# A hybrid decoder step: the reciprocal of lambda's squared modulus made early and kept

## The chip, the cores and the metric

One core of one Trainium2 chip runs the kernel, which is written by hand for its five engines (TensorE, VectorE, ScalarE, GpSimd, and SyncE, which issues loads). The metric is the device time of one execution in microseconds, as the median of three runs. Nothing is computed on the host.

## The reference, cut to what matters

The program is one inference step of a two-layer decoder for 256 prompt tokens and 8 x 4 sample tokens, together 288 columns. Layer 0 has forgetting attention and an S5 state-space layer side by side behind one input projection, then an output projection and a SwiGLU feed-forward part. Layer 1 has a pooling mixer and a feed-forward part. The change concerns the constants of S5:

```python
def s5_mixer(u, h0_re, h0_im, lam_re, lam_im, log_dt, b_re, b_im, c_re, c_im, d, w_glu, b_glu):
    dt = jnp.exp(log_dt.astype(F32))[:, None]
    lr, li = lam_re.astype(F32), lam_im.astype(F32)
    mag = jnp.exp(lr * dt)
    ar, ai = mag * jnp.cos(li * dt), mag * jnp.sin(li * dt)
    den = lr * lr + li * li
    zr = ((ar - 1.0) * lr + ai * li) / den
    zi = (ai * lr - (ar - 1.0) * li) / den
    ...
    # bb = z * b; a scan x <- a x + bb u over the tokens; y = Re(c x) + d u
    z = jax.nn.gelu(y)
    out = z * jax.nn.sigmoid(z @ w_glu.astype(F32) + b_glu.astype(F32))
```

There are 64 groups of 64 states, so den, zr and zi are arrays of 128 partitions x 32 on the chip.

## The kernel before, in words

**The weight stream.** All large products take their weights from a ring. SyncE loads a unit of 256 KB into one of four raw buffers; ScalarE casts it to float32r (wh, line 124), VectorE makes the rest (wl = raw - wh, line 125), and TensorE makes three products for each tile (lines 162 to 164: wh with xh, wh with xl, wl with xh). A unit of layer 0's projections has 12 such matmuls over 288 columns. There are four buffers of wh and wl, and the split of a unit is put into the queues three units ahead of its products.

**Ticks.** After the products of each unit the program, as it is written out, calls tick(): each generator in the list side goes one step further and puts its instructions into the engines' queues there. So the order of each engine's queue is fixed by hand: a table W says how many ticks ("units of products") pass between two steps that wait for one another, and ticks(n) lets n of them pass. Engines work through their queues in order; an instruction whose operands are late holds up all behind it on that engine. Where a part needs a flag that is not set yet, until(...) calls ticks with no products between (forced ticks).

The order of the stream in layer 0 is: u (4 groups of 8 units, ticks 1 to 32), f (33), q and k (8 groups of 8, ticks 34 to 97), v (4 groups of 8, to 129), GLU (16 units), w_out's S5 half of two groups (8 units), until the prompt's and the samples' attention is done, then the rest of w_out.

**S5.** gen_s5_prep makes the constants, nearly all on GpSimd, in small steps of 128 x 32: exp32 of log_dt and of lambda times dt, sine and cosine by polynomials, powers of a, then den, am = ar - 1, zr, zi. Then VectorE makes z times b (the tile tab at line 194), and the powers of a times b and c (powers). TensorE makes the lag matrix (L585), which goes through eight small DMAs (L607) into mt. gen_s5_main brings u into place, makes the states (L726, then GpSimd steps and fill), and the outputs (L784), writes y to zscr and loads it again as zs (L805), from which the GLU takes its input zt. gen_s5_direct makes the part of y within a chunk from mt.

Counted in the code, the steps of before fall on these ticks:

| step | tick |
|---|---|
| first S5 step (exp32 of log_dt) | 1 |
| den and am put into GpSimd's queue | 6 |
| reciprocal of den put into VectorE's queue | 15 |
| zr, zi and the step factors put into GpSimd's queue | 16 |
| first products with b (tab) in VectorE's queue | 19 |
| states begin (flag g), end of them (flag gdone) | 48, 68 |
| fill begins | 83 |
| mt there (flag m), direct part done (flag direct) | 88, 93 |
| prompt heads begin, two chains of four heads, 14 ticks a head | 103, 105 |
| load of zs issued (flag z) | 125 |
| GLU asks for z | 129 |
| transposes of heads 6 and 7; their products with v | 152, 154; 157, 159 |
| w_out asks for the attention: six forced ticks | 155 to 161 |

The flag direct also starts the prompt's attention (through gen_cb and its ticks). The samples' attention follows q and k: its first three tiles of key pages (two loads of 256 KB each) are asked for at gdone, one more each second tick from 77 on; pages of v in the same way from 125 on.

small(...) and t2(...) hand out tiles; t2 is a ring of five buffers of one tag. In exp32 the tile named den is scratch, too.

Of the kernel before, what the change touches and what calls it, by code (L numbers as in the profile page):

```python
# [15 lines left out]
# units of products that pass between steps that wait for one another  # L16
W = dict(n0a=3, n0b=0, n0c=0, n0d=2, rec=9, s5a=3, gq=0, xw=0, qk0=2, qk1=2, qk2=0, qk3=1, qk4=0, f=2, m=4, lag=2,
# [44 lines left out]
def hybrid_step(ctx, tc, I, O):  # L62
# [9 lines left out]
    # ---------------------------------------------------------------- helpers  # L72
# [24 lines left out]
    class Ring:  # L97
        """weights: loaded, split into two float32r parts that add up to them, handed out in order"""
# [45 lines left out]
    def group(ring, ks, kpu, rhs, nb=2, m=128, evac=None, ps=None, first=True, last=True, pre=None, n=NT):  # L144
        """nb blocks of m output features: sum over the tiles of ks of weights times rhs"""
        if ps is None:
            ps = psum.tile([128, 2, 512], F32, name="m", tag="m", bufs=2)
        pb = ps if isinstance(ps, list) else [ps[:, b] for b in range(2)]
        c = nb * m
        ks = list(ks)  # L150
        for u in range(0, len(ks), kpu):
            if pre is not None:
                pre(u // kpu)
            h, l = ring.take()
            for j, k in enumerate(ks[u:u + kpu]):
                xh, xl = rhs(k)
                for b in range(nb):
                    o = pb[b][:m, :n]
                    w0 = j * c + b * m
                    st = first and u + j == 0  # L160
                    sp = last and u + j == len(ks) - 1
                    T.matmul(o, h[:, w0:w0 + m], xh, start=st, stop=False)  # L162
                    T.matmul(o, h[:, w0:w0 + m], xl, start=False, stop=False)  # L163
                    T.matmul(o, l[:, w0:w0 + m], xh, start=False, stop=sp)  # L164
            ring.ahead(ring.look)
            tick()
            if u + kpu >= len(ks) and evac is not None:
                pending.append(lambda: evac(ps))
        return ps
# [10 lines left out]
    def use_table(func):  # L180
        """Ln and Exp from the set that has both"""
        if func in (AF.Ln, AF.Exp):
            if table[0] != "ln_exp":
                S.preload_act_table_set("natural_log_exp_and_others")
            table[0] = "ln_exp"
        else:
            table[0] = func
# [14 lines left out]
    # ------------------------------------------------------ constants, inputs  # L202
# [13 lines left out]
    # ------------------------------------------------------------- rms norms  # L216
    class Norm:
        """xh + xl = x * w in two parts, and rstd, which products are scaled by"""
# [62 lines left out]
    def rsqrt_steps(srcs, n, out):  # L281
        """out[:, i] = (srcs[i] / n + eps) ** -0.5"""
        c = len(srcs)
        v = t2("v", shape=(128, c, NT))
        y = t2("y", shape=(128, c, NT))
        q = t2("q", shape=(128, c, NT))
        for i, s in enumerate(srcs):
            V.tensor_scalar(v[:, i, :], s, 1.0 / n, EPS, op0=OP.mult, op1=OP.add)
        yield
        act(y, v, AF.Ln)  # L290
        act(y, y, AF.Exp, scale=-0.5)
        S.activation(q, y, AF.Square)
        yield
        V.scalar_tensor_tensor(q, q, -0.5, v, op0=OP.mult, op1=OP.mult)
        if isinstance(out, list):
            out.append(q)
            out = q
        V.scalar_tensor_tensor(out, q, 1.5, y, op0=OP.add, op1=OP.mult)

    # ======================================================= layer 0: mixers  # L300
# [5 lines left out]
    def w_units(ap, kpu):  # L306
        """ap: [groups, 128, k tiles, c]"""
        out = []
        for g in range(ap.shape[0]):
            for k in range(0, ap.shape[2], kpu):  # L310
                a = ap[g, :, k:min(k + kpu, ap.shape[2])]
                out.append(a.rearrange("p k c -> p (k c)"))
        return out

    def first_two(units, order=(0, 1, 2, 4, 5, 6, 3, 7)):
        """the units of two groups of 16 k tiles, interleaved, 4 tiles each time"""
        n = len(units) // 8
        u = [units[i * n:i * n + n] for i in range(8)]
        return sum([u[i] for i in order], [])
# [28 lines left out]
    def gen_n0():  # L348
        """squares, their sums, and the first outputs, which wait for them"""
        yield from ticks(W["n0a"])  # L350
        sq = None
        for j in range(8):
            if sq is not None:
                add(n0.acc, n0.acc, sq)
            sq = n0.square(j, False)
            yield
        G.dma_start(bcd[:, 0], I["s5b"])
        G.dma_start(bcd[:, 1], I["s5c"])
        add(n0.acc, n0.acc, sq)
        n0.combine(V)  # L360
        yield from ticks(W["n0b"])
        n0.finish_pe(psum)
        yield from ticks(W["n0c"])
        for _ in n0.finish_steps():
            yield from ticks(W["n0d"])
        yield
        flags.add("rstd")
        for f, ps in early:
            f(ps)
            yield  # L370
        flags.add("early")
# [7 lines left out]
    # ------------------------------------------------ S5: constants of layer  # L379
# [6 lines left out]
    def gstt(out, a, c, b, op0, op1):  # L386
        """out = (a op0 c) op1 b"""
# [5 lines left out]
    def exp32(out, x):  # L393
        """exp on [128, 32]: 2**n times a polynomial, to the last bits"""
# [13 lines left out]
    def gen_s5_prep():  # L408
        lre, lim, ldt = (par[:, o:o + 32] for o in (P_LRE, P_LIM, P_LDT))
        dt, th, mag = small("dt"), small("th"), small("mag")  # L410
        exp32(dt, ldt)
        yield
        mul(mag, lre, dt, G)
# [3 lines left out]
        # sin and cos of th: the angle brought into [-pi, pi], then a polynomial  # L417
# [43 lines left out]
        am, den, t, u = small("am"), small("den"), small("zt"), small("zu")  # L461
        zr, zi = small("zr"), small("zi")
        mul(den, lre, lre, G)
        mul(t, lim, lim, G)
        add(den, den, t, G)
        G.tensor_scalar(am, ar, -1.0, None, op0=OP.add)
        yield from ticks(W["rec"])
        V.reciprocal(den, den)
        yield
# [3 lines left out]
        mul(zr, t, den, G)  # L473
# [3 lines left out]
        mul(zi, t, den, G)  # L477

        def steps(name, a):
            """the factors of a step, laid out as the states are: quarters, parts, pairs"""  # L480
# [44 lines left out]
        def powers(dst, src, j0, pr, neg):  # L525
            """dst[:, part, pair, j] = src * a**(j0 + j); the imaginary part negated if neg"""
# [47 lines left out]
        # lags: kall[64 h2 + c', quad, g2, (j, c)]  # L574
# [58 lines left out]
    # ------------------------------------------------------------- u, and f  # L633
# [49 lines left out]
    def gen_s5_main():  # L683
# [10 lines left out]
        # states: initial ones of the samples, zeros, ends of the chunks of the prompt  # L694
# [8 lines left out]
        def step(eng, dst, src, a, sh):  # L703
            """dst += a * src; sh: how many of them, of how many pairs"""
# [13 lines left out]
        for q in range(4):  # L718
# [14 lines left out]
            # within blocks of 4 chunks  # L733
# [6 lines left out]
        # the ends of the blocks, one after the other  # L740
# [8 lines left out]
        def fill(eng, q):  # L749
            """what the blocks start from, carried through their chunks"""  # L750
# [57 lines left out]
    def gen_s5_direct():  # L808
        """the part of y within a chunk"""
# [28 lines left out]
    # ------------------------------------------------ f: the logs of forgetting  # L838
# [41 lines left out]
    # ---------------------------------------------------------------- q and k  # L880
# [40 lines left out]
    # ----------------------------------------------------- attention: samples  # L921
# [99 lines left out]
    def gen_prep(hg):  # L1021
        """probabilities of the samples, keys first, on the columns of their products"""
# [76 lines left out]
    # ----------------------------------------------------- attention: prompt  # L1099
    def gen_prompt(e):  # L1100
        yield from need("cb")
        yield from ticks(W["ps0"] * e)
        for h in range(e, NH, 2):
# [28 lines left out]
            # keys 0: queries 0, queries 1; keys 1: queries 1  # L1132
# [31 lines left out]
    # -------------------------------------------------------------------- v  # L1164
# [46 lines left out]
    # ------------------------------------------------------------------- glu  # L1211
# [34 lines left out]
    # ----------------------------------------------------------------- w_out  # L1246
# [31 lines left out]
    # =================================================================== ffn  # L1278
# [69 lines left out]
    # ============================================================== pooling  # L1348
    # the windows are sums over tokens: they are taken after the products, of
    # columns 0 .. 287 and, of what the state brings to a window, 288 .. 319  # L1350
# [57 lines left out]
    def before_last():  # L1408
        """before the last products of the ffn of layer 0"""
# [76 lines left out]
    def gen_pool_out():  # L1486
        """the last inputs of the pooling, which are outputs too"""
# [13 lines left out]
    def pool_and_first(h_evac):  # L1501
        """the products of the pooling, among them the first two groups of the ffn"""
# [53 lines left out]
def layouts(inp):  # L1556
# [21 lines left out]
    def gp(v):  # L1578
        """[64 groups, 64 states, ...] -> [128, 32, ...]"""
# [26 lines left out]
    def blocks(w, c):  # L1606
        """[K, M] -> [M / c, 128, K / 128, c]"""
# [59 lines left out]
```

## Time and profile before

| | |
|---|---|
| median of 3 runs | 2233.71 us (2233.02 to 2234.71) |
| span of the profiled execution | 2232.2 us |
| TensorE matmuls busy | 2176.1 us, 97% |
| VectorE busy | 1251.3 us, 56% |
| ScalarE busy | 911.6 us, 41% |
| GpSimd busy | 244.7 us, 11% |
| DMA | 375.50 MB, mean 168 GB/s |

The profile is of one execution. A busy share is an average over the whole span; what one place costs is read from the timelines of that place. A row of a timeline gives the start in us from the start of the span, the duration in us, the engine, the line of the code, the operation with the tiles that it writes and reads, and in brackets how long its engine stood idle before it and what ended that. In rows PE is TensorE, DVE is VectorE, ACT is ScalarE, POOL is GpSimd, SP is SyncE; a q behind the name is the engine's queue of DMA issues. PEclk is the granted clock as a share of 2.4 GHz. Ends of matmuls are modelled.

### The profile page before, as it was taken

To read this page: it belongs to the slowest core of one execution; us is meant where nothing else is said; L and a number is where in the kernel's file an instruction comes from. 1 tells how busy PE (TensorE), PEld (TensorE's weight loads), DVE (VectorE), ACT (ScalarE), POOL (GpSimd) and SP (SyncE) were. 2 spreads that over 40 slices of the span, in tenths; PEclk is the share of its full clock that TensorE was granted. 3 is DMA by queue.
4 is the path that set the end of the run, shared out by engine and by line. 5 is a ranking of instruction groups with operands and counts; after the bars stand their busy time and mean duration, and the time that the engine had idled before them with its cause. 6 is when DMAs were issued, how large, how long until landed. Compare 5 with 4: busy or idle time off the path is not lost.

```text
span 2232.2 us, 40924 instructions
## 1 busy us (share of the span) xinstructions
PE 2176.1 (97%) x16936; PEld 2138.3 (96%) x16936; DVE 1251.3 (56%) x1616; ACT 911.6 (41%) x1302; POOL 244.7 (11%) x321
## 2 busy tenths in 40 slices
PE   8998999999999999999999996899999999999999
PEld 7987988999999999999999996899999999999999
DVE  6987656655554544554554569655554455445443
ACT  5454545444333333333333353433333333333332
POOL 8365200100000000000000046200000000000000
PEclk9999999999999999999999999999999999999999
DMA  6638487555555555555555642455556555555554
GB/s 201 170 106 198 133 250 253 186 189 170 168 163 167 161 171 164 168 161 171 163 167 159 202 150 86 158 169 162 168 158 169 168 168 162 169 164 168 159 170 140
DMA packets 136571, 375.50 MB, mean 168 GB/s; under 512 B 22337, under 2 KB 26129, under 8 KB 136097
## 3 DMA queue, kind: packets, MB, share of 16 engines
q1 hardware_dynamic: 122864, 357.15, 53.1%
q10 hardware_dynamic: 11728, 11.27, 1.6%
q0 software_dynamic: 1792, 4.47, 0.7%
q8 instruction: 132, 2.16, 0.4%
q14 instruction: 55, 0.44, 0.1%
HBM read 363.42 MB, written 8.76 MB: 167 GB/s over the span
## 4 chain that ended last, share of the span: by engine, by line
PE 88%; DVE 5%; DMA 3%; POOL 2%; ACT 1%; issue 1%; ACTq 0%; SPq 0%; DVEq 0%
PE m L164 28%; PE m L162 28%; PE m L163 28%; DVE wb L197 1%; DVE wl L125 1%; PE s L784 1%; POOL stt L390 1%; DMA raw<-in_wqk_dram 1%; DMA zs<-zscr 0%; ACT wh L124 0%; DVE wb L194 0%; PE s L726 0%; PE a L585 0%; DMA raw<-in_wv_dram 0%; DMA raw<-in_w_dram 0%
## 5 line engine op out<-in xcount | busy, mean ns | idle before, releaser
L125 DVE TENSOR_TENSOR wl<-raw,wh 128x1024 fp32r<-128x1024 f32 (+2 forms) x758 | 808.1, 1071 | 793.3 <-ACT wh L124 790.2
L124 ACT CAST wh<-raw 128x1024 fp32r<-128x1024 f32 (+2 forms) x769 | 691.2, 903 | 940.0 <-PE m L163 751.7
L162 PE MATMUL m<-xh,wh 128*128 128x288 f32 (+1 forms) x3312 | 985.2, 297 | 19.0 <-ACT xh L234 12.6
L164 PE MATMUL m<-xh,wl 128*128 128x288 f32 (+1 forms) x3312 | 982.9, 297 | 16.3 <-DVE wl L125 10.4
L163 PE MATMUL m<-xl,wh 128*128 128x288 f32 (+1 forms) x3312 | 982.2, 297 | 0.0
L162 PEld LDWEIGHTS m<-xh,wh 128*128 128x128 f32 (+1 forms) x3312 | 623.9, 188 | 28.0 <-ACT xh L234 13.1
L164 PEld LDWEIGHTS m<-xh,wl 128*128 128x128 f32 (+1 forms) x3312 | 624.2, 188 | 20.4 <-DVE wl L125 13.0
L163 PEld LDWEIGHTS m<-xl,wh 128*128 128x128 f32 (+1 forms) x3312 | 624.5, 189 | 1.5 <-DVE xl L235 0.5
L164 PE MATMUL m<-gh,wl 128*128 128x288 f32 x1408 | 415.8, 295 | 0.0
L163 PE MATMUL m<-gl,wh 128*128 128x288 f32 x1408 | 415.5, 295 | 0.0
L162 PE MATMUL m<-gh,wh 128*128 128x288 f32 x1408 | 414.1, 294 | 0.0
L164 PEld LDWEIGHTS m<-gh,wl 128*128 128x128 f32 x1408 | 264.4, 188 | 0.0
L162 PEld LDWEIGHTS m<-gh,wh 128*128 128x128 f32 x1408 | 264.4, 188 | 0.0
L163 PEld LDWEIGHTS m<-gl,wh 128*128 128x128 f32 x1408 | 264.4, 188 | 0.0
L191 ACT ACTIVATE s<-t 128x288 f32<-128x288 f32 x88 | 39.1, 445 | 169.2 <-DVE t L194 169.2
L1359 POOL DMA_DIRECT2D out_plo_dram<-es x1 | 0.6, 577 | 779.8 <-DMA es<-in_spool_dram 779.8
L194 DVE TENSOR_TENSOR t<-s,t 128x288 f32<-128x288 f32 x88 | 40.3, 457 | 46.4 <-ACT s L191 46.4
L194 DVE TENSOR_TENSOR t<-m,rstd 128x576 f32<-128x576 f32 x88 | 65.9, 749 | 0.0
L1313 DVE TENSOR_TENSOR gl<-t,gh 128x288 fp32r<-128x288 f32 x88 | 40.3, 458 | 44.0 <-ACT gh L1312 44.0
L197 DVE TENSOR_TENSOR x<-m,x 128x576 f32<-128x576 f32 x72 | 54.0, 750 | 8.6 <-PE m L164 8.6
L1312 ACT CAST gh<-t 128x288 fp32r<-128x288 f32 x88 | 38.2, 434 | 46.1 <-DVE t L194 46.1
L197 POOL TENSOR_TENSOR acc<-acc,sq 128x576 f32<-128x576 f32 x20 | 31.7, 1583 | 196.9 <-ACT sq L244 186.6
(338 smaller groups left out, 1490.8 us busy)
## 6 DMA issues: line engine op xcount, KB each, us to landing
raw<-in_w_dram SPq DMA_DIRECT2D x472, 512.0 KB, 4.0
raw<-in_w_dram SPq DMA_DIRECT2D x64, 384.0 KB, 3.2
raw<-in_wqk_dram SPq DMA_DIRECT2D x64, 256.0 KB, 3.2
raw<-in_wout_dram SPq DMA_DIRECT2D x64, 256.0 KB, 3.2
raw<-in_wu_dram SPq DMA_DIRECT2D x32, 256.0 KB, 3.8
pg<-in_kc_dram SPq DMA_DIRECT2D x32, 256.0 KB, 3.7
raw<-in_wv_dram SPq DMA_DIRECT2D x32, 256.0 KB, 3.4
pg<-in_vc_dram SPq DMA_DIRECT2D x28, 256.0 KB, 3.9
```

Source lines behind the costliest of these rows:

```text
L124: S.copy(h[:, :n], t[:, :n])
L125: self.share().tensor_tensor(l[:, :n], t[:, :n], h[:, :n], OP.subtract)
L162: T.matmul(o, h[:, w0:w0 + m], xh, start=st, stop=False)
L163: T.matmul(o, h[:, w0:w0 + m], xl, start=False, stop=False)
L164: T.matmul(o, l[:, w0:w0 + m], xh, start=False, stop=sp)
L191: S.activation(out, x, func, **kw)
L194: eng.tensor_tensor(out, a, b, OP.mult)
L197: eng.tensor_tensor(out, a, b, OP.add)
L390: G.tensor_scalar(t, a, c, None, op0=op0)
L784: T.matmul(ps[64 * h2:64 * h2 + 64, 72 * d:72 * d + 72], p0[k, pair, r, 16:80], xt[k, 0:72, q, r, pair - 8 * q], start=r == 0, stop=r == 1)
L1312: S.copy(gs[c][0][:, i, :], t[:, 1, :])
L1313: V.tensor_sub(gs[c][1][:, i, :], t[:, 1, :], gs[c][0][:, i, :])
```

## The change

The squares and the sum that make lambda's squared modulus move from the end of GpSimd's chain to its head, ahead of the first exp32, into a tile of their own (rden) with a scratch tile from t2 (sqi). The reciprocal moves with them: VectorE's instruction is put in its queue in the second step of gen_s5_prep, and its result is kept until zr and zi need it. The step between the reciprocal and zr goes (one tick less), and W["rec"], the ticks that pass ahead of zr, becomes 13 in place of 9. Comments and docstrings are dropped as well, which changes no instruction.

```diff
-W = dict(n0a=3, n0b=0, n0c=0, n0d=2, rec=9, s5a=3, gq=0, xw=0, qk0=2, qk1=2, qk2=0, qk3=1, qk4=0, f=2, m=4, lag=2,
+W = dict(n0a=3, n0b=0, n0c=0, n0d=2, rec=13, s5a=3, gq=0, xw=0, qk0=2, qk1=2, qk2=0, qk3=1, qk4=0, f=2, m=4, lag=2,
...
     def gen_s5_prep():
         lre, lim, ldt = (par[:, o:o + 32] for o in (P_LRE, P_LIM, P_LDT))
+        rden, sqi = small("rden"), t2("sqi", shape=(128, 32))
+        mul(rden, lre, lre, G)
+        mul(sqi, lim, lim, G)
+        add(rden, rden, sqi, G)
         dt, th, mag = small("dt"), small("th"), small("mag")
         exp32(dt, ldt)
         yield
+        V.reciprocal(rden, rden)
         mul(mag, lre, dt, G)
         exp32(mag, mag)
...
         ar, ai = ap[:, 1, 0, :], ap[:, 1, 1, :]
-        am, den, t, u = small("am"), small("den"), small("zt"), small("zu")
+        am, t, u = small("am"), small("zt"), small("zu")
         zr, zi = small("zr"), small("zi")
-        mul(den, lre, lre, G)
-        mul(t, lim, lim, G)
-        add(den, den, t, G)
         G.tensor_scalar(am, ar, -1.0, None, op0=OP.add)
         yield from ticks(W["rec"])
-        V.reciprocal(den, den)
-        yield
         mul(t, am, lre, G)
         mul(u, ai, lim, G)
         add(t, t, u, G)
-        mul(zr, t, den, G)
+        mul(zr, t, rden, G)
         mul(t, ai, lre, G)
         mul(u, am, lim, G)
         G.tensor_tensor(t, t, u, OP.subtract)
-        mul(zi, t, den, G)
+        mul(zi, t, rden, G)
```

## Rows read from the trace of the kernel before

**Rows 1.** The page of the profiled execution, its head.

```profile
span 2232.2 us, 40924 instructions
```

**Rows 2.** Windows around the reciprocal: busy us (instructions), clock, DMA share, GB/s.

```profile
37.15:42.05 4.90, 4.89 (x38) 4.66 (x36) 0.00 (x0) 1.64 (x3) 4.13 (x16) 1.00 0.22 68
42.05:46.98 4.93, 0.00 (x0) 0.00 (x0) 0.95 (x3) 0.00 (x0) 4.36 (x15) 0.97 0.00 0
46.98:50.00 3.02, 3.02 (x12) 3.02 (x13) 2.99 (x8) 0.00 (x0) 2.69 (x8) 0.50 0.75 221
```

**Rows 3.** VectorE's timeline: start, us, line, operation, idle before and releaser.

```profile
46.03 0.35 DVE L468 RECIPROCAL den<-den 128x32 f32<-128x32 f32 x1 [8.89 <-POOL den L197]
46.30 0.63 DVE L125 TENSOR_TENSOR wl<-raw,wh 128x512 fp32r<-128x512 f32 x1
...
52.20 0.69 DVE L194 TENSOR_TENSOR tab<-bcd,zr 128x512 f32<-128x512 f32 x1
```

**Rows 4.** Timelines of ScalarE and TensorE, 312 to 327 us.

```profile
312.95 0.38 ACTq L805 DMA_DIRECT2D zs<-zscr  x1
...
323.91 3.25 ACT L1219 CAST zt<-zs 128x512 fp32r<-128x512 f32 x5 [1.74 <-PE a L1059]
...
319.21 0.65 PE L1059 MATMUL a<-pg,vtp 128*32 128x128 f32 x16
...
325.24 0.40 PE L162 MATMUL m<-zt,wh 128*128 128x288 f32 x1 [0.58 <-ACT zt L1219]
```

**Rows 5.** DMA from 309 to 326 us: whole mean, then issues (us to landing).

```profile
DMA packets 2719, 4.26 MB, mean 251 GB/s; under 512 B 197, under 2 KB 1221, under 8 KB 2718
...
raw<-in_wglu_dram SPq DMA_DIRECT2D x5, 256.0 KB, 5.8
pg<-in_vc_dram SPq DMA_DIRECT2D x5, 256.0 KB, 4.5
zs<-zscr ACTq DMA_DIRECT2D x1, 1152.0 KB, 10.9
```

**Rows 6.** DMA from 165 to 210 us, the same view.

```profile
DMA packets 7833, 9.04 MB, mean 201 GB/s; under 512 B 3728, under 2 KB 3728, under 8 KB 7797
...
mt<-kall ACTq DMA_DIRECT2D x2, 128.0 KB, 6.9
```

**Rows 7.** Waits from 171 to 208 us: total us, times, longest.

```profile
ACT wh L124 <- DMA raw<-in_wqk_dram: 15.3, 6, 5.0
...
PE s L899 <- DVE sl L893: 3.9, 1, 3.9
...
DVE tms L755 <- POOL car L759: 2.6, 1, 2.6
```

**Rows 8.** Timelines of TensorE and ScalarE, 380 to 390 us.

```profile
383.60 0.27 PE L1134 MATMUL s<-cst,sm 128*128 128x128 f32 x1
...
385.52 0.59 PE L1142 MATMUL s<-sm,vtp 128*128 128x256 f32 x2
...
384.19 0.47 ACT L1138 COPY sm<-s 128x384 f32<-128x384 f32 x1
```

**Rows 9.** GpSimd's timeline, 2 to 51 us.

```profile
2.88 0.22 POOL L397 TENSOR_SCALAR am<-par 128x32 f32<-128x32 f32 x1 [2.41 <-DMA par<-in_par_dram]
...
11.68 0.50 POOL L391 TENSOR_TENSOR dt<-stt,ei 128x32 f32<-128x32 f32 x1
...
12.68 0.32 POOL L397 TENSOR_SCALAR am<-mag 128x32 f32<-128x32 f32 x1
...
24.10 0.50 POOL L391 TENSOR_TENSOR mag<-stt,ei 128x32 f32<-128x32 f32 x1
...
46.20 0.77 POOL L357 DMA_DIRECT2D bcd<-in_s5b_dram  x1
...
50.57 0.25 POOL L194 TENSOR_TENSOR zi<-zt,den 128x32 f32<-128x32 f32 x1
```

**Rows 10.** DMA from 40 to 70 us, issues (us to landing).

```profile
bcd<-in_s5b_dram POOLq DMA_DIRECT2D x1, 512.0 KB, 4.0
```

## Prediction

> **What bounds the kernel now.** The profiled execution spans 2232.2 us [rows 1], 1.5 us under the median of the timed runs (2233.71). I make the sum against the span and add 1.5 at the end. A difference of 0.2%, 4.5 us, is about what a measurement of this kernel can tell from no change.
>
> I read the page first: TensorE is the bound nearly everywhere, so only the few places where it stands still can give or take time. Then I went through TensorE's gaps with the chain of waits beside them, up to the feed-forward part that begins near 400 us (behind it no gap is long and the S5 work is over). Four places matter.
>
> First, the reciprocal. In the windows [rows 2] the reader sees three stretches: TensorE full, then 4.93 us with no matmul at all, then 12 matmuls in 3.02 us at granted clock 0.50, the lower of its two levels (1.2 GHz). At full clock 38 matmuls fill 4.90 us, so 12 take 1.55 us. The VectorE line shows why [rows 3]: the reciprocal stood 8.89 us at the head of VectorE's queue, for GpSimd's sum of squares, which comes last in GpSimd's chain. Behind it stood the split of unit 19, which TensorE needed. The place costs 4.93 + (3.02 - 1.55) = 6.4 us.
>
> Second, the end of the S5 path [rows 4]. The load of zs is issued at 312.95, lands 10.9 us later [rows 5], the casts start at 323.91 and the first GLU product at 325.24 after a gap of only 0.58. So the S5 path is just in time: zs lands as TensorE runs out of v products.
>
> Third, 171 to 208 us: the DMA engines are saturated (201 GB/s over 165 to 210 us [rows 6]), ScalarE waits 15.3 us for raw weights, and TensorE waits 3.9 us for one split of a q/k square [rows 7]. Fourth, the start of w_out's attention half, behind the products with v at 385.52 [rows 8].
>
> **The change, part by part.** The sum of squares moves to the head of GpSimd's chain. A step of this size takes 0.22 to 0.50 us there [rows 9]; three go in at the head and three go out at the tail, so the chain's end stays. The reciprocal itself (0.35 us [rows 3]) now stands in tick 2, behind work that needs far more time than GpSimd's three steps; even if nothing hid it, 0.35 us is its price. I take 0. The scratch tile sqi takes one place in a ring of five whose tile of five places earlier is long read: 0. So the 8.89 us wait goes, and with it up to 6.4 us at this place.
>
> The second edit is the one to weigh. Formerly 9 ticks, then the reciprocal, then one more step: GpSimd's zr/zi chain stood in tick 16 and VectorE's first product with it (tab) in tick 19. Now 13 ticks pass and no step of its own for the reciprocal: tick 19 and tick 22. Everything behind in S5 moves by three ticks: m from 88 to 91, direct 93 to 96, z 125 to 128; the prompt heads, which start on direct, move with it. The weight stream does not move, and GLU still asks for z in tick 129. So the load of zs, which had four more units of v products as its cover, has one left.
>
> I therefore follow the S5 path, not TensorE, from tab to the GLU.
>
> (a) When tab starts. Without the stall TensorE ends unit 18 at 42.05 and runs on at 1.6 us a unit (12 matmuls); unit 25, the last split ahead of tab, ends at 42.05 + 7 x 1.6 = 53.2, and VectorE reaches tab near 48 (unit 25 takes the buffer of unit 21, which TensorE ends at 42.05 + 4.8 = 46.9; a cast and a split of 0.63 us [rows 3] follow). But tab needs zr and bcd. GpSimd issues the first bcd load at 46.20 and it lands 4.0 us later, 50.2; zi is there at 50.57 + 0.25 = 50.8 [rows 9, 10]. These do not come earlier through the change, since they stand behind the whole chain. They may come later: the chain's stretch from 37.15 to 46.20 now runs beside a busy VectorE, where before VectorE stood still (0.00 busy from 37.15 to 42.05 [rows 2]). The two passes of the same exponential give the price: from the am row at 2.88 to the end of dt, 9.3 us, from the am row at 12.68 to the end of mag, 11.9 us [rows 9], 28% more, with VectorE much busier in the second. On 9.05 us that is up to 2.5; I take 2.0. Then tab starts at 52.2, where it started before (52.20). Shift 0, bounds -2.0 (no slowing) and +0.5. So of the 8.89 us VectorE keeps a new wait of some 4 us for GpSimd and bcd. Unit 26's split follows the two products, near 54.3, 1.1 us after TensorE ended unit 25: a small gap returns, already inside this term.
>
> The Trainium skill speaks against the change here (SBUF — State Buffer, section Who interferes with whom): a VectorE instruction with two SBUF inputs and a GpSimd instruction that reads SBUF exclude one another for a whole instruction. The two passes above agree in direction. If each of some six splits in the stretch held GpSimd up for its full 0.63 us, the chain would end 3.8 us later in place of 2.0, an estimate from that page, and the time would be 2236.7 in place of 2234.9.
>
> (b) From tab to the issue of zs there are 106 ticks before and after, with as many products, the same S5 and prompt work. What stands in ticks 126 to 128 in place of 19 to 21 is denser: sample products with v pages, 0.65 us each [rows 4], one every second tick: 1.5 x 0.65 = +1.0. Bounds 0 and +2.
>
> (c) In the saturated stretch the mt writes, 6.9 us for 128 KB [rows 6], and the first burst of key pages move by three ticks, but the later page loads do not (they follow q and k). About 1.5 tiles of two 256 KB loads more fall into it: 0.77 MB at 201 GB/s, 3.8 us if all of it shows, nothing if the ticks ahead of it absorb them. It is nearer to nothing, since only part of the stretch stops TensorE: +0.8.
>
> (d) zs now lands beside fewer weight and page loads. Before, some 7 of the 11 loads of 256 KB in that window ran beside its 1152 KB at 251 GB/s [rows 5]. Each load less saves 0.26 MB / 251 GB/s = 1.0 us. Those already in flight stay, the ring fills its four raw buffers all the same; I take one, -1.0, bounds -4 and 0.
>
> (e) The w_out wait. Heads 6 and 7 have their transposes in ticks 152 and 154, ahead of the last product unit's tick 155, and their products with v in forced ticks behind it. Three ticks later all of the transposes, copies and products stand behind the last unit. After the last product the row at 385.52 has to wait for a transpose and its copy: 384.19 - 383.60 = 0.59 from one to the other, and 0.47 for the copy [rows 8], with a tenth of handing on 1.2 us. Bounds 0 and +2.6 (with twelve matmuls at the lower clock behind it, another 1.4).
>
> (f) The q/k square that waited 3.9 us stood behind the first carries of fill, which waited for GpSimd [rows 7]. Heads of q/k do not move, fill moves three ticks, so they part. But ScalarE was short of weights in the same stretch (15.3 us), so little of it is free: -0.8; bounds 0 and -5.4 (the 3.9 and 1.5 for twelve matmuls at the lower clock behind it, as at 47 us).
>
> Sum: 0 + 1.0 + 0.8 - 1.0 + 1.2 - 0.8 = +1.2. The 6.4 us at the reciprocal are won, and paid back by TensorE in front of the GLU: it comes there some 5 us earlier and waits for zs, 5 to 7 us in place of the 0.58 of [rows 4]. Span 2232.2 + 1.2 = 2233.4, median 2233.4 + 1.5 = **2234.9**.
>
> **Rivals.** One, faster: the gain is kept. Either zs comes much sooner, or TensorE's lead lets the collision of (f) vanish. For it: zs alone would need 1.18 MB / 251 GB/s = 4.7 us, and the wait of (f) is real. Against it: the weights in flight, and the starved ScalarE. At the full bound of (f), 4.6 us less than my value, and (d) at -3, 2 us less, the median is 2234.9 - 6.6 = 2228.3. It decides from the point where GLU's first product starts before 319.5.
>
> Two, slower: the page loads meet the mt writes. Place: VectorE's and ScalarE's wait for raw weights between 171 and 208 us. Price: (c) at its bound, 3.0 over my value, and (f) gone, 0.8, and zs as slow as before, 1.0, since the late pages then run into it: 2234.9 + 4.8 = 2239.7. It decides once ScalarE's waits for raw weights in this stretch grow from 15.3 to about 19 us.
>
> Three: the reciprocal waits as before, in tick 2, and nothing is removed. It would need GpSimd's first three steps to be late; they need only the load that the row at 2.88 waited for. Then the stall at 42 us stays, and the shift costs three ticks at the GLU; from 312.95 to 325.24 there are five units [rows 4], 2.5 us each, so 7.4 us, and with (e) 2242. I give it under 1 in 50.
>
> **How the numbers follow.** Forecast (paid back, within 0.2%) 0.62; rival one 0.16; rivals two and three together 0.22. So faster 0.16, same 0.62, slower 0.22. The range leaves out about a tenth on each side and reaches to the first two rivals: 2228.3 to 2239.7.
>
> **What will show it.** Step one is right if no reciprocal waits on GpSimd near 46 us and TensorE runs through 42 to 47 at full clock. (a) is right if tab starts between 50.2 and 52.7 and waits for zr or bcd. The payback is right if the first GLU product starts within 3 us of 325.24 with a gap of 5 us or more ahead of it. (e) shows as a gap between the last ssmh product and the first att product. I am wrong if the GLU starts near 319 (gain kept), or near 330 (S5's stretch became longer); the places to look are then [rows 4] and [rows 7].

## The result, and the profile after

The changed kernel takes 2246.47 us in the median of 4 runs (2243.78 to 2249.63), against 2233.36 us before: ratio 1.006, 95% interval 1.0049 to 1.0072. It is slower by some 13 us, and outside the range that was forecast. The profiled execution took 2247.39 us, 13.4 us of span more than [rows 1]:

```profile
span 2245.6 us, 40926 instructions
PE 2183.6 (97%) x16936; PEld 2143.6 (95%) x16936; DVE 1250.4 (56%) x1616; ACT 913.8 (41%) x1302; POOL 245.8 (11%) x321
```

The wait that was to go is gone. VectorE's timeline after, beside [rows 3]:

```profile
11.60 0.35 DVE L417 RECIPROCAL rden<-rden 128x32 f32<-128x32 f32 x1
46.80 0.69 DVE L125 TENSOR_TENSOR wl<-raw,wh 128x512 fp32r<-128x512 f32 x1 [0.89 <-ACT wh L124]
55.24 0.69 DVE L194 TENSOR_TENSOR tab<-bcd,zr 128x512 f32<-128x512 f32 x1 [7.74 <-DMA bcd<-in_s5b_dram]
55.86 0.69 DVE L194 TENSOR_TENSOR tab<-bcd,zi 128x512 f32<-128x512 f32 x1
56.47 0.69 DVE L125 TENSOR_TENSOR wl<-raw,wh 128x512 fp32r<-128x512 f32 x1
```

The reciprocal no longer waits, but VectorE stands 7.74 us before tab in place of 8.89 before the reciprocal, and the next split is again what TensorE needs. Windows of the profile after, beside [rows 2] (busy us and instructions by engine, then clock, DMA share, GB/s):

```profile
core 0: us, PE busy (x) PEld busy (x) DVE busy (x) ACT busy (x) POOL busy (x), PEclk, DMA share, GB/s
42.00:46.00 4.00, 4.00 (x32) 4.00 (x32) 2.82 (x7) 1.35 (x3) 3.49 (x7) 1.00 0.83 268
57.22:60.30 3.08, 3.08 (x13) 3.08 (x14) 3.08 (x5) 0.00 (x0) 2.92 (x6) 0.50 0.44 126
```

TensorE runs through the place of the old stall at full clock, stands still ten microseconds later, and comes back at the lower clock (1.2 GHz), 13 matmuls in 3.08 us. GpSimd's timeline after says why, beside [rows 9]:

```profile
3.37 0.25 POOL L197 TENSOR_TENSOR rden<-rden,sqi 128x32 f32<-128x32 f32 x1
3.71 0.22 POOL L397 TENSOR_SCALAR am<-par 128x32 f32<-128x32 f32 x1
13.99 0.31 POOL L391 TENSOR_TENSOR dt<-stt,ei 128x32 f32<-128x32 f32 x1
28.00 0.67 POOL L391 TENSOR_TENSOR mag<-stt,ei 128x32 f32<-128x32 f32 x1
51.38 0.77 POOL L357 DMA_DIRECT2D bcd<-in_s5b_dram  x1
54.80 0.25 POOL L194 TENSOR_TENSOR zi<-zt,rden 128x32 f32<-128x32 f32 x1
```

The chain begins 0.8 us later, is 4 us late at mag, and issues bcd at 51.38 where it was 46.20. TensorE's timeline after, its three long waits:

```profile
57.22 0.61 PE L164 MATMUL m<-xh,wl 128*128 128x288 f32 x1 [4.40 <-DVE wl L125]
188.13 0.73 PE L998 MATMUL a<-pg,qm 128*32 128x256 f32 x8 [4.53 <-POOL xt L711]
334.96 0.61 PE L162 MATMUL m<-zt,wh 128*128 128x288 f32 x1 [5.65 <-ACT zt L1219]
```

The second is the first product with a key page; the third is the GLU waiting for zs, 9.7 us later than in [rows 4]. ScalarE's timeline after, the way of z:

```profile
324.38 0.38 ACTq L805 DMA_DIRECT2D zs<-zscr  x1
333.71 4.38 ACT L1219 CAST zt<-zs 128x512 fp32r<-128x512 f32 x8 [6.50 <-DMA zs<-zscr]
```

The load of zs goes out 11.4 us later than in [rows 4], and takes 9.3 us to the first cast in place of 11.0. From the first product with att, that is, with the attention's output in w_out, the two kernels run alike again: 1846.2 us to the end after, 1845.5 before.

### The profile page after: what moved, and what is told of

The parts are those of the page before. It is cut to its first block, busy times and chain, and to the rows that moved or that the text cites. A ratio compares the mean times of both kernels' runs of the same rounds, so it can differ in the third digit from the quotient of the medians.

```text
span 2245.6 us, 40926 instructions
## 1 busy us (share of the span) xinstructions
PE 2183.6 (97%) x16936; PEld 2143.6 (95%) x16936; DVE 1250.4 (56%) x1616; ACT 913.8 (41%) x1302; POOL 245.8 (11%) x321
## 4 chain that ended last, share of the span: by engine, by line
PE 86%; DVE 5%; POOL 3%; DMA 2%; ACT 1%; issue 1%; SPq 0%; ACTq 0%; DVEq 0%; POOLq 0%
PE m L162 28%; PE m L164 28%; PE m L163 28%; DVE wl L125 1%; DVE wb L197 1%; PE s L784 1%; POOL xt L711 1%; POOL stt L390 1%; DMA raw<-in_w_dram 1%; ACT wh L124 1%; DMA pg<-in_vc_dram 0%; DVE wb L194 0%; POOL tms L707 0%; DMA zs<-zscr 0%; DMA raw<-in_wqk_dram 0%
## 5 line engine op out<-in xcount | busy, mean ns | idle before, releaser
L164 PE MATMUL m<-xh,wl 128*128 128x288 f32 (+1 forms) x3312 | 984.8, 297 | 13.4 <-DVE wl L125 9.5
L164 PEld LDWEIGHTS m<-xh,wl 128*128 128x128 f32 (+1 forms) x3312 | 626.3, 189 | 17.4 <-DVE wl L125 11.9
```

## The experiments

The table gives, for each profiled execution, the starts of three rows of the timelines (tab, issue of zs, first GLU product with the wait ahead of it, first product with att) and the median of its timed runs; the ratio to before, with its interval, stands at each run below.

| kernel | tab | zs issued | GLU (wait) | att | median us |
|---|---|---|---|---|---|
| before | 52.20 | 312.95 | 325.24 (0.58) | 386.74 | 2233.36 |
| changed | 55.24 | 324.38 | 334.96 (5.65) | 399.39 | 2246.47 |
| early_rec10 | 53.65 | 314.90 | 327.11 (0.50) | 388.57 | 2233.98 |
| shift_alone | 56.24 | 325.67 | 336.76 (6.17) | 401.35 | 2249.38 |
| late_back3 | 52.65 | 316.56 | 328.67 (0.36) | 389.86 | 2236.51 |
| cb5 | 53.18 | 323.64 | 334.77 (6.57) | 397.89 | 2245.56 |
| no_acc_adds | 52.15 | 322.37 | 333.83 (6.53) | 397.32 | 2248.42 |
| rec16 | 54.02 | 316.47 | 328.11 (7.19) | 394.94 | 2244.32 |
| rec16_back6 | 54.28 | 309.48 | 323.19 (2.00) | 384.93 | 2232.24 |
| best13 | 50.37 | 316.63 | 329.20 (0.86) | 390.36 | 2235.76 |
| best_rec10 | 49.43 | 311.33 | 323.87 (0.82) | 385.05 | 2231.20 |
| best10_pg | 49.61 | 313.56 | 326.28 (1.01) | 387.86 | 2232.59 |

### Each edit alone

**early_rec10**: the early reciprocal without the shift (S5 in the ticks of before).

```diff
-rec=13
+rec=10
```

> The early reciprocal alone: 10 ticks in place of 13, so that zr stands in tick 16 and tab in tick 19, as in the kernel before. Theory A (the loss is S5 standing three ticks later in a weight stream that has no lead over it by the time it counts): z is back in tick 125, the first GLU product starts within 4 us of 325, and the time is 2231 to 2238; VectorE waits at tab for zr and bcd from about 44 us on. Theory B (the loss is GpSimd's chain, which now ends 5 us later and sets S5's start in data; ticks do not matter): tab at 55, GLU near 335, 2243 to 2247. On the chain itself: if it is VectorE's work beside it that makes it late, it ends at 47 to 49 us here, since VectorE stands from 44 on; if it is the three steps at the head alone, it ends at 51 as in the changed kernel.

Measured: 2233.98 us (11 runs), ratio 0.9999 (0.999 to 1.0008), as theory A has it. VectorE's timeline of early_rec10:

```profile
53.65 0.69 DVE L194 TENSOR_TENSOR tab<-bcd,zr 128x512 f32<-128x512 f32 x1 [10.35 <-POOL zi L194]
```

The early reciprocal alone is worth nothing that can be measured: VectorE waits at tab in place of the reciprocal, and TensorE then waits 7.66 us for the next split. From the changed kernel this one differs in three ticks alone, and the 13 us of loss are gone. On the chain neither reading came true: it ends at 50.0, between the two.

**shift_alone**: the kernel before, its late reciprocal kept, with three ticks more ahead of tab.

```diff
-s5a=3
+s5a=6
```

> The kernel before with its late reciprocal, and three more ticks between zr and tab, so that tab stands in tick 22 and all of S5 behind it three ticks later. The stall of 8.9 us at the reciprocal stays, GpSimd's chain ends at 46 as before. Theory A: 2242 to 2248, the first GLU product at 332 to 337. Theory B: chain and zr as before, so 2232 to 2236.

Measured: 2249.38 us (4 runs), 1.0076 (1.0061 to 1.0091). TensorE's and VectorE's timelines of shift_alone:

```profile
46.83 0.61 PE L164 MATMUL m<-xh,wl 128*128 128x288 f32 x1 [6.02 <-DVE wl L125]
45.88 0.35 DVE L468 RECIPROCAL den<-den 128x32 f32<-128x32 f32 x1 [10.15 <-POOL den L197]
336.76 0.61 PE L162 MATMUL m<-zt,wh 128*128 128x288 f32 x1 [6.17 <-ACT zt L1219]
```

The old stall is there, and the GLU's new wait too. The shift alone costs at least as much as the whole change (the two intervals overlap): with early_rec10 this shows that the shift is the loss.

**late_back3**: the changed kernel, three ticks given back ahead of S5's outputs and ahead of the prompt heads.

```diff
-p=9, cb=8
+p=6, cb=5
```

> The changed kernel, with three ticks taken out of S5's later waits (6 in place of 9 between the direct part and the outputs; 5 in place of 8 in front of the prompt's heads), so that z is in tick 125 and the prompt heads are in ticks 103 and 105 again, while tab stays in tick 22. Theory A: the GLU's wait of 5.7 us goes, first GLU product at 324 to 329, 2232 to 2238. Theory B: the outputs wait for their data instead, GLU near 333 to 335, 2242 to 2247.

Measured: 2236.51 us (12 runs), 1.0018 (1.0009 to 1.0027). 10 of the 13 us come back with the program at the head left as it was: the loss is where z and the heads stand in the order. **cb5** gives back the heads' ticks alone (cb=5):

> The changed kernel with the prompt heads' start three ticks earlier (5 in place of 8 ticks behind the direct part), so that they stand in ticks 103 and 105 again; z stays in tick 128. Theory A: the part between the first GLU product and the first product of w_out with att, 61.5 us before and 64.4 with the change, is 61 to 62 again, and the time is 2 to 4 us below the change: 2242 to 2245. If the part stays at 64 the heads are not what w_out waits for, and the time stays at 2246.

Measured: 2245.56 us (4 runs), 1.0058 (1.0043 to 1.0074). From the first GLU product to the first with att it takes 63.1 us, before 61.5, changed 64.4, so theory A's 61 to 62 is missed and little of the loss is the heads'. cb5 and late_back3 differ in p alone, and have tab at 53.18 and 52.65: with z three ticks earlier its load goes out 7.1 us sooner and the time is 9 us shorter. So late_back3's gain is nearly all that of p, thus of z.

### The head: does the late chain decide?

**den_vector**: the two squares and the sum on VectorE.

```diff
-        mul(rden, lre, lre, G)
-        mul(sqi, lim, lim, G)
-        add(rden, rden, sqi, G)
+        mul(rden, lre, lre)
+        mul(sqi, lim, lim)
+        add(rden, rden, sqi)
```

> The changed kernel, with the two squares and their sum on VectorE in place of GpSimd (VectorE stands idle at that time), so that GpSimd's chain has neither the three steps at its head nor at its tail. Theory A1 (the head steps make the chain late: they push the exponentials by 0.85 us into a stretch in which VectorE is busy, and more grows out of it): the first exponential starts at 2.9 in place of 3.7, the chain ends at 46 to 48.5 in place of 48.9 to 51.4, tab starts at 50 to 52.5, TensorE's stall near 57 shrinks from 4.4 to under 2, and the time is 2238 to 2244, since S5 still stands three ticks late. Theory A2 (the lateness comes only from VectorE no longer standing still after 37): the chain ends only about 0.8 earlier, 48.1 to 50.6, and the time is as with the change.

Measured: 2245.88 us (4 runs), 1.006 (1.0045 to 1.0076). The chain starts at 2.81 again and is 1.0 us late at mag, not 4, but am stands at 49.72, still 3.8 us late: what is lost behind mag is lost without the three steps too. The time is as theory A2 has it, and TensorE still waits 3.32 us near 57.

**no_acc_adds**: the changed kernel without six of the seven additions n0.acc += sq on VectorE; so part of the norm's sum is left out. It ran once.

```diff
-            if sq is not None:
-                add(n0.acc, n0.acc, sq)
```

> The changed kernel without six of the seven sums of squares of the first norm on VectorE (sums of two tiles in SBUF, 0.8 us each, 18 to 31 us), so the norm's sum lacks them. If VectorE's two-input work slows GpSimd's steps beside it, the second exponential (dt to mag), 13.9 to 14.4 us with the steps at the head, takes 11 to 12.5, and the chain ends 1.5 to 3.5 us earlier, at 46 to 49. If GpSimd's pace is its own, both stay: 13.9 to 14.4, chain end 48.9 to 51.4. The time is not the point: 2238 to 2246.

Measured: 2248.42 us. The second exponential takes 11.9 us (dt's end to mag's; changed 14.4, before 12.4), am is at 47.83, the earliest of ten executions in which GpSimd does the squares, and tab starts at 52.15, as before. TensorE waits only 2.33 us there. Yet the GLU comes at 333.83 after 6.53 us, and the time of this one run is no better. cb5 against early_rec10 says the same with more runs: tab at 53.18 and 53.65, and 2245.56 against 2233.98 us. So tab's lateness is not what costs.

**rec16**: three ticks more still, so that VectorE comes to tab when bcd is there.

```diff
-rec=13
+rec=16
```

> The changed kernel with 16 ticks in place of 13: tab in tick 25, z in tick 131, behind the tick in which the GLU asks for it. Theory A: VectorE hardly waits at tab and TensorE has no stall near 57 us, yet the time is longer again by 2.5 to 3 us a tick: 2252 to 2257, GLU near 343. Theory B: what counts is when zr and bcd are there, so 2244 to 2249 as with 13. A side question: whether the weight stream keeps the lead that it has without the stall; if the raw weights set its pace from 75 to 100 us, the first split of a q/k square (L893) still starts within 2 us of 101.8, if not it starts near 97.

Measured: 2244.32 us (4 runs), 1.0057 (1.0042 to 1.0071). TensorE has no wait at tab, and its stream is 8.8 us ahead near 100 us (the split of the first q/k square at 93.09; 101.84 before, 102.02 changed). Theory A missed: three ticks more cost nothing more. The load of zs now stands behind the tick in which the GLU asks for it, where the ticks are forced and hold no products, and near 308 us the stream is still 7.3 us ahead, where with 13 it is some 4 us late. This is the payback that the prediction described: the GLU comes 2.9 us after [rows 4], and waits:

```profile
328.11 0.61 PE L162 MATMUL m<-zt,wh 128*128 128x288 f32 x1 [7.19 <-ACT zt L1219]
```

But from there to att it takes 66.8 us in place of 61.5, with 4.9 us in place of 1.5 without a matmul; with the heads' six ticks given back (rec16_back6 below) it takes 61.7.

### The first key pages

The wait at 188.13 carries GpSimd's name, but the product starts 0.10 us behind the end of VectorE's copy of qm, as it also does in late_back3_pg below (180.82 + 0.25 to 181.17). SyncE's, ScalarE's and VectorE's timelines after show what holds that copy:

```profile
174.88 6.07 SPq L949 DMA_DIRECT2D pg<-in_kc_dram  x6
184.69 0.62 ACT L124 CAST wh<-raw 128x512 fp32r<-128x512 f32 x1 [5.63 <-DMA raw<-in_wqk_dram]
185.34 0.84 DVE L125 TENSOR_TENSOR wl<-raw,wh 128x512 fp32r<-128x512 f32 x1 [2.56 <-ACT wh L124]
187.78 0.25 DVE L985 COPY qm<-qn 128x128 f32<-128x128 f32 x1
```

Six page loads in one go hold SyncE's queue for 6.07 us; ScalarE is out of raw weights for 5.63; the split waits for it, and behind that split stands the copy of qm, which the page products need. Before, the burst stood at 164.71, three units further ahead of this copy, and the product hardly waited. The same row of before:

```profile
182.57 0.64 PE L998 MATMUL a<-pg,qm 128*32 128x256 f32 x8 [0.67 <-POOL xt L711]
```

**late_back3_pg**: late_back3, the first three tiles asked for one at a time; only SyncE's order changes.

```diff
-        ahead()
+        ahead(1); yield; yield; ahead(2); yield; yield; ahead()
...
-            yield from ticks(W["sc0"])
+            yield from ticks(W["sc0"] if hg else 1)
```

(The last line makes up for the ticks that the new yields take, so that copy and page products keep their place.)

> This is the changed kernel with p=6 and cb=5 (2236.5 us, with 5.04 us of TensorE waiting at the first product with a key page), and only SyncE's queue changed: the first three tiles of key pages are asked for one at a time, two ticks apart, in place of six loads in one go, so weight loads come in between. Theory A: the burst of six loads keeps the raw weights 6 us from ScalarE, and the copy of qm, which the page products need, stands on VectorE behind the split that waits for them. Then the wait at the first page product falls under 2 us, and the time to 2232.5 to 2235. Theory B: the products wait for the pages, or for GpSimd's states, as the record of the wait names it: the wait stays at 4 to 6 us, and the time at 2236 to 2238.

Measured: 2237.84 us (11 runs), 1.0018 (1.001 to 1.0027), the same as late_back3. The timeline of late_back3_pg:

```profile
170.71 1.51 SPq L949 DMA_DIRECT2D pg<-in_kc_dram  x2
176.29 1.48 SPq L949 DMA_DIRECT2D pg<-in_kc_dram  x2
181.17 0.64 PE L998 MATMUL a<-pg,qm 128*32 128x256 f32 x8 [1.73 <-POOL xt L711]
```

The mechanism is as theory A has it (the wait was 5.04 us in late_back3), but its time is not, it wins none: at the first page product TensorE is 3.7 us ahead of late_back3, at 310 us 1.6, and the two spans differ by 0.4 (2233.9 and 2234.3). The same on two kernels told of below: **best13_pg**

> best13 with the first key pages asked for one tile at a time, two ticks apart. Theory A: the wait at the first page product falls under 2 us, and the time is 2 to 4 us below that of best13, 2226 to 2230, if the GLU does not wait for zs. Theory B (z sets the end): what is won at the pages is waited away at the GLU, with a gap of 3 us or more, and the time is within 1 us of that of best13.

with 2233.02 us (12 runs), 1.0001 (0.9993 to 1.001), against best13's 1.0009, intervals that overlap: the wait falls from 4.60 to 1.74 us, and the time lies between the two theories; and **best10_pg**, on best_rec10 (without the line on sc0; its page products stand at the same place),

> The version of 2231.2 us (rec=10, the squares on VectorE, bcd loaded by SyncE) with the first three tiles of key pages asked for one at a time, two ticks apart; their products not moved. Theory A (in the saturated stretch the burst of pages holds weights up, and that reaches the end): 2228 to 2230.5. Theory B (the S5 path sets the pace behind it): within 1 us of 2231.2, with the GLU's first product again near 323.9.

with 2232.59 us (11 runs), 0.9996 (0.9987 to 1.0005), against 2231.2, and the GLU at 326.28: no gain, against theory A. In one of three, best13_pg, it may win some 2 us.

**late_back3_sc7** moved copy and page products three ticks later:

```diff
-sc0=4
+sc0=7
```

> The same kernel with p=6 and cb=5, and the copy of qm and all products with key pages three ticks later (sc0=7 in place of 4), the page burst left as it is. Theory A (weights held up by the burst): the copy no longer stands behind the starved split, but the starved split itself stops TensorE's weight products for 1 to 3 us: 2233.5 to 2236. Theory B (the pages or the states are late for their first use): the wait at the first page product goes below 1 us with nothing in its place: 2231.5 to 2233.5. Both wrong: the later page products delay the samples' attention, and it is slower than 2236.5.

Measured: 2244.83 us (4 runs), 1.0056 (1.0041 to 1.0072): the third case. The GLU comes at 327.80, but the samples' attention is late, and TensorE waits 4.14 us for its probabilities at 348.88.

### Is TensorE's lead real?

**best13**: squares on VectorE, bcd loaded by SyncE, rec=13, p=6, cb=5.

```diff
-        G.dma_start(bcd[:, 0], I["s5b"])
-        G.dma_start(bcd[:, 1], I["s5c"])
+        SY.dma_start(bcd[:, 0], I["s5b"])
+        SY.dma_start(bcd[:, 1], I["s5c"])
```

> The changed kernel with the two squares and the sum on VectorE, the loads of bcd issued by SyncE in place of GpSimd (2231.2 us with rec=10), rec=13 kept, and p=6 and cb=5 that give the three ticks back later. Theory A (the stall at tab was GpSimd's late chain, and the shift costs only by its later ticks): tab starts between 49 and 51, TensorE waits under 1.5 us there, its stream is 3 to 6 us ahead of the kernel before from there on, the first page product waits 4 to 6 us again, and the time is 2229 to 2233. Theory B (z sets the end whatever the head does): the GLU waits 3 us or more for zs and the time is 2232 to 2236.

Measured: 2235.76 us (10 runs), 1.0009 (1.0 to 1.0018). Tab is at 50.37 and TensorE waits under 1 us near it; the stream is 5.3 us ahead at 95 us, and 3.7 behind at 310. The first page product waits 4.60 us, as theory A has it, but the time is theory B's, and the GLU waits only 0.86 us, so B's reason is missing too.

**rec16_back6**: rec16 with all six ticks given back (p=3, cb=2).

> The same with all six ticks given back, p=3 and cb=2: load of zs and start of the heads in the ticks of the kernel before, states, fill and direct part six ticks later than there. Theory A: the GLU's first product between 318 and 323, the first att product between 379 and 385, and the time 2226 to 2232, clearly below before. Theory B: 2233 or more: the steps of S5 that are now closer together wait for one another, or the work put off is done in front of the GLU.

Measured: 2232.24 us (11 runs), 0.9994 (0.9985 to 1.0003). Windows of rec16_back6 between the first and the fourth pair of q/k blocks, and from there to the eighth:

```profile
87.94:143.23 55.29, 52.44 (x550) 48.62 (x550) 51.10 (x94) 33.10 (x70) 23.79 (x23) 1.00 0.45 132
143.23:253.26 110.03, 101.75 (x1068) 91.01 (x1068) 80.14 (x132) 53.41 (x94) 61.19 (x84) 0.94 0.56 163
```

Between the same points TensorE did 777 and 848 matmuls before. Of the 15.1 us that the stream is ahead at 143, 7.6 arise in the first stretch, with 227 matmuls fewer in it: S5 work put off, done in the second. The other 7.5 us, the lead at the head, are real, and half of them are lost in the second stretch, which ran at granted clock 0.94 (before 0.97). 3.5 us are left at 310 us, and 2.0 at the GLU, which waits 2.00 us for zs. So theories A and B each have a part. **rec16_back3** gives back three ticks (p=6, cb=5):

> The changed kernel with rec=16 (2244.3 us; no wait of TensorE at tab, its stream 8.8 us ahead near 100 us and still 6 to 7 ahead near 310 us; then 7.2 us of waiting for zs at the GLU and 5.3 more at w_out), and three of its six ticks given back with p=6 and cb=5. Theory A (TensorE's lead is real and is only waited away, because z and the heads stand later in the order): the GLU's first product comes between 320 and 324 with a gap under 3 us, the first att product between 382 and 388, and the time is 2229 to 2235. Theory B (the lead is only side work put off, which TensorE does later, so nothing is to be had): 2236 or more, with the GLU near 328 as with p=6 and rec=13.

Measured: 2241.3 us (5 runs from 2235.26 to 2244.03), 1.0036 (1.0022 to 1.005). The profiled run, its fastest, has the GLU at 325.07 after 5.25 us of waiting, later than theory A and sooner than theory B; the median lies in theory B's range, but its runs differ too much to tell more.

**best_rec10**: rec=10, squares on VectorE, bcd by SyncE.

> A version that may beat both: squares, sum and reciprocal early on VectorE, 10 ticks so that S5 stands in the ticks of the kernel before, and the two loads of bcd issued by SyncE's queue in place of GpSimd's, so that tab waits for zr alone and GpSimd does not spend 1.3 us on the issues. Theory A: the chain ends near 46 to 48, zr is there 2.5 us later, tab starts at 48 to 51 in place of 53.7 with the early reciprocal on GpSimd alone, TensorE's stall at that place is 3 to 5.5 us in place of 7.7, and the time is 2228 to 2232. Theory B (S5's start does not reach the end): 2233 to 2235 as with the early reciprocal alone.

Measured: 2231.20 us (11 runs), 0.999 (0.9981 to 0.9999): just faster than before by its interval, and the best of all. Zi ends at 51.1, so tab starts 2.8 us sooner, and the issue of zs and the GLU 1.6 and 1.4 us. That the earlier tab is the reason is not shown: best10_pg has tab at 49.61 too, and issues zs 0.6 us later than before.

## Why the prediction was wrong

**The reciprocal, the scratch tile, TensorE through 42 to 47 us: right.**

**(a), the start of tab: wrong in size.** The chain's end came 5.2 us late, not 2.0 (bound 2.5); tab at 55.24, not 52.2; TensorE waited 4.40 us, not 1.1, and then ran at the lower clock. The first output of f's unit 33 came at 79.92 against 80.83: 0.9 us are left of the 6.4. Ten executions with the squares at the head of GpSimd's chain, no_acc_adds among them, have the last am between 47.83 and 51.14 (45.96 before), so 2 to 5 us late: the profiled one is the latest, and the bound of 2.5 was too narrow. The estimate from the Trainium skill (SBUF — State Buffer, section Who interferes with whom), 3.8 us, lies inside this. The trace agrees in direction (the chain ended 5.2 us late beside a VectorE that no longer stood still); no run isolates the exclusion of whole instructions.

**(b), tab to the issue of zs: the step that failed.** It was put at +1.0 and was 324.38 - 55.24 - (312.95 - 52.20) = +8.4. The ticks left out lie in the head, where one lasts 1.6 us. Those taken on lie ahead of the GLU: from the last page product there to the issue of zs it takes 324.38 - 314.12 = 10.3 us, before 312.95 - 309.89 = 3.1, so 2.4 us each, 7.2 for the three. The prediction priced them like the ticks of the head with 1.0 us on top, and trusted that TensorE's gain at 47 us would still stand at 310, where the stream is 4.2 us late (314.12 against 309.89). Rival three had the price, 7.4 us for three ticks at the GLU and 2242 us, but tied it to a reciprocal that waits.

Followed by TensorE the sum is plain: the stream is 0.9 us ahead near 80 us, loses 5.2 between 95 and 310, and is 4.2 late; three ticks later, 7.2 us, the load of zs goes out, 11.4 late in all; the faster load gives back 1.6, and the GLU is 9.7 late. The loss in the middle comes with the shift as well: without it, in early_rec10, the stream loses 0.7 us there (from 96.70 to 311.80, before from 95.47 to 309.89). That the shift does this, and not the late tab, is shown by early_rec10 and shift_alone, which have each edit alone, and by cb5 and late_back3, which differ in z's ticks alone. A lead at the head does not save it: in rec16 it is waited away, in best13 it is gone by 310 us.

**(c), pages: the stretch right, cause and price not.** It was put at 0.8 us for more bytes in the saturated stretch. From 171 to 208 us the DMA engines moved 204 GB/s after and 202 before, and ScalarE's waits for raw weights fell from 15.3 to 9.1 us, so rival two's sign (19 us) did not come. What came is one wait of 4.53 us, at a place not foreseen: the copy of qm behind the starved split. Taking that wait away brought no time that could be measured, so its share of the loss is not shown.

**(d), the load of zs: right in size by luck**, 1.6 us faster for 1.0 forecast. The reason given, fewer loads beside it, is not what the traces show: from the issue of zs to the first cast, weights and pages took 1.82 MB after and 1.79 before; all loads together moved at 322 in place of 272 GB/s. Why is open.

**(e), w_out: right in direction, not in reason**, 2.9 us from GLU to att for 1.2. The wait that it priced is 0.24 us, at 398.06. 2.8 of the 2.9 us are busy time: 62.79 us for 575 matmuls in place of 59.99 for 571, at a granted clock of 0.94 in place of 0.97. From 334.96 to 338.64, behind the wait for zs, the clock is 0.50. In late_back3, where the GLU waits 0.36 us, it is 1.00 from GLU to att, and 572 matmuls take 58.83 us.

**(f), the q/k square: right.** The wait of 3.86 us [rows 7] is gone, and with the shift: in early_rec10 it is there, 6.05 us. Waits of 1.93 and 1.29 us at 218.95 and 236.39 stand in its place.

**The payback: wrong as a mechanism.** The GLU does wait over 5 us for zs, but at 335, past the 330 that was named as the sign that S5's stretch became longer. And it is no gain waited away: TensorE ends the last matmul ahead of the GLU at 329.3, before at 324.7, so it came 4.7 us later, not 5 earlier.

Still open: why the same instructions on GpSimd end up to 2.5 us apart from one execution to the next (the end of this text shows what their passes go with), and what takes the 2 us that late_back3_pg loses again between the pages and 310 us.

## What to carry to other kernels

Where the order is written out by hand, a step that is moved by three units carries every flag behind it along; price the shift in units at the last place that asks for the flag, not at the place where it was made, and see whether these units hold products there (in rec16 the last ones hold none, and three ticks more cost nothing more). A stall that one late chain causes is not removed by taking one of its waiters away: look for the next instruction in the queue that needs the same chain. Before a gain at the head is counted, see whether the stream still has it at the last meeting with the other path, and how much of it is work put off.

## What was not expected of the hardware

The same small GpSimd steps of an exponential (128x32) took 9.3 us in the first pass of before and 13.6 us in the second of the changed kernel (15.04 to 28.67). Leaving out six VectorE additions shortened the time from dt's end to mag's from 14.4 to 11.9 us, while the first pass of that run took 11.5 us. Both go with VectorE's busy time beside the pass. The first pass took 9.30 us where VectorE was busy for 4.09 us of it (before), 10.59 at 6.62 (changed) and 11.47 at 7.67 (no_acc_adds); the second 11.40 at 8.03 (no_acc_adds), 11.92 at 11.45 (before) and 13.64 at 13.05 (changed). Over all 17 executions a straight line through these pairs gives some 0.5 us more for each us of VectorE's, in either pass, an estimate from these rows. A longer pass also takes in more of VectorE's work, and no run isolates which of that work it is.

Stalls cost twice: from the first pair of q/k blocks to the last page product of the keys (95 to 310 us before) TensorE's matmuls were busy 204.1 us before and 207.7 us after (2116 and 2109 of them), since the stretches behind waits ran at a lower granted clock, as 57.22 to 60.30 above at 0.50, and 188.13 to 191.80, behind the page wait, at 0.56; over the first 65 us of this stretch it was 0.95, before 1.00. Of the 5.2 us that the stream loses there, 3.6 are longer busy time for nearly as many matmuls, which I put down to the clock, and 1.6 are waits.
